# SBUF places of a hybrid attention kernel: small tiles collected in pools of their own, tables padded, 280-column weights spread

## The chip, the core and the metric

The kernel runs on one core of a Trainium2 chip. The core has a matrix engine (TensorE, called PE in the profile; the loading of its stationary operand is shown apart as PEld), three elementwise engines (VectorE = DVE, ScalarE = ACT, GpSimd = POOL) and DMA queues, most of which are issued here from SyncE (SP). All work on SBUF, a memory of 128 partitions; a tile takes the same byte range in every partition, and "place" below means the first byte of a tile, or of a slice of it, within its partition. Matmul results go to PSUM. The metric is device time in microseconds (us) from launch to end, the median of several executions.

## What is computed

One layer of a decoder trunk in float32, 1024 tokens of width 1024. Cut to its steps:

```python
h = rmsnorm(x, norm_mix)
q, kc, vc, ks, vs, kw, vw, nsa_g, rq, rk, rv, rg, gate_a, gate_b = split(h @ w_in)
A = nsa(...)        # compressed + selected + sliding-window attention, gated per head
B = retention(...)  # chunkwise recurrent, per-head norm, swish gate
x = x + (sigmoid(gate_a) * (A @ w_proj_a) + sigmoid(gate_b) * (B @ w_proj_b)) @ w_out
x = x + relu(rmsnorm(x, norm_mlp) @ w_up) ** 2 @ w_down
y = rmsnorm(x, norm_final)
```

## The kernel before

**Matmuls.** Every float32 matrix is split into a high and a low part of type fp32r (`wh`, `wl` for weights; `bh`, `bl` for the transposed activations), and a product is three matmuls: high·high, high·low, low·high. All go through the helper `mm` (L156, its instruction is L157), whose second argument is the stationary operand (loaded into the array) and whose third is the moving one (streamed, up to 512 columns). Before each matmul PE loads the stationary 128x128 block. While one matmul streams, the next one's load runs.

**Stages, in the order of time.** The names in brackets are the PSUM tiles by which the profile's rows tell the stages apart.

- Normalization, retention projections and retention, twice four column groups (`mm`, and small ones `pS`, `pO`, `pD`, `pZ`): `dense_tok` (L218) holds `bh`/`bl` stationary and streams weights of 512 columns. Then the keys and values of attention (w_kva, 512 columns; w_kvb, 280 columns) and the queries (w_q, 512), also `mm`, with the compression matmuls `pc` between them.
- Attention (`S` scores, `pt` transposes of the probabilities, `O` the value products of 256 columns), interleaved with the merge gates (`gps`, weights stationary, `bh`/`bl` moving). The order here is a list of pieces with due times (L934 to L953).
- Projections of A and B (`mm` of L1010; moving tiles `Ah`, `Al`, `Bh`, `Bl`, weights stationary).
- Output product (`mmu` with `bh`/`bl` stationary and w_out moving), with the transposes that form the input of the MLP.
- MLP up (`mmu`, seven products for a pair of blocks in `up_rest`; weights stationary; moving `bh`, `bl` and the sums `t2h`..`t4l`).
- MLP down (`mmd`, `three`, L1294; both operands are `wh`/`wl` tiles of the weight ring).

PE takes its instructions in the order in which they are written. The other engines' lists are ordered by the tile framework. Weights come by DMA into `raw` (3 buffers, L160), are copied to `wh` on ACT and the rest subtracted into `wl` on DVE (`split_w` L181, `split_t1024` L1027).

**Places.** Pools are stacked from the low end of SBUF, some (`side="right"`) from the high end. A tile's size is rounded up to 32 bytes, so a small tile shifts all that is stacked above it. In the build of the kernel before, the 128-column identity `ident` starts at byte 16512, and behind it stand the small tiles `small`, `nhalf`, `gcol`, `ssx` and `rr` (224 bytes with rounding); `raw` therefore starts at 17248. `cret` (2848 bytes), `cmp_m` (480 bytes) and the score scratch tiles `sums`, `mx`, `cf` shift what stands above them again. `chunk_weights` (L228) packs two weight blocks of n columns next to each other; for n = 280 the second block starts 1120 bytes behind the first.

Byte address of the matmul operands modulo 256, from the allocations of the two builds (slices step by multiples of 256 bytes except the packed 280-column blocks):

| operand | before | after |
|---|---|---|
| `bh`, `bl`, `t2h`..`t4l`, `KKs`, `KKw`, `KKc`, `Vs`, `Vw`, `Vc`, `qkT` (right side) | 224 | 224 |
| weights `wh`, `wl` in the ring of the whole kernel, and in the rings of the later stages | 96 | 224 |
| weights `wh`, `wl` in the retention ring (`wrx`) and the compression ring | 128 | 224 |
| second 280-column block in a 96 ring, in a 128 ring | 192, 224 | 224 |
| `Ah`, `Al`, `Bh`, `Bl` | 96 | 224 |
| `QQ`, `ql`, `pS`, `pW` | 64 | 224 |
| `ph`, `pl` | 192 | 224 |
| `ident`, retention tiles (`qk`, `s`, `v`, `sd`, `n`, `z`), compression tiles (`xh`, `xl`, `w2d`, `hh`) | 128 | 224 |
| x rows that are transposed for the MLP (`x1t`), `AT` | 96 | 224 |

Of the 5552 fp32r matmuls with 512 columns, the two operands of 1728 agree modulo 256 before (384 of the projections and 1344 of MLP down, all at 96), and those of 3824 don't: 1152 `mm` of `dense_tok`, 768 `gps`, 176 `S`, 384 `mmu` of the output product, 1344 `mmu` of MLP up. After, the operands of all 7879 PE instructions agree, at 224.

Of the kernel before, what the change touches and what calls it, by code (L numbers as in the profile page):

```python
# [9 lines left out]
F32 = mybir.dt.float32  # L10
F32R = mybir.dt.float32r
I32 = mybir.dt.int32
AF = mybir.ActivationFunctionType
OP = mybir.AluOpType
# [3 lines left out]
P = 128  # L18
S = 1024
D = 1024  # L20
NT = S // P
KD = D // P
# [90 lines left out]
def hybrid_block(ctx: ExitStack, tc: tile.TileContext, a: dict, out: bass.AP):  # L113
    nc = tc.nc
    V, A, G, T = nc.vector, nc.scalar, nc.gpsimd, nc.tensor
    ctx.enter_context(tc.manual_schedule(engines={mybir.EngineType.PE}))

    cst = ctx.enter_context(tc.tile_pool(name="cst", bufs=1, reuse_waits="tile"))
    dram = ctx.enter_context(tc.tile_pool(name="scr", bufs=1, space=DRAM))
    bigs = ctx.enter_context(ExitStack())  # L120
    big = bigs.enter_context(tc.tile_pool(name="big", bufs=1, side="right", reuse_waits="tile"))
    wraw = ctx.enter_context(tc.tile_pool(name="wraw", bufs=3, reuse_waits="tile"))
# [8 lines left out]

    bh = big.tile([P, KD, S], F32R, name="bh")
    bl = big.tile([P, KD, S], F32R, name="bl")
    ident = cst.tile([P, P], F32, name="ident")
    small = cst.tile([P, 16], F32, name="small")
    nhalf = cst.tile([P, 4], F32, name="nhalf")
    gcol = cst.tile([P, KD], F32, name="gcol")
    ssx = cst.tile([P, 2, NT], F32, name="ssx")
    rr = cst.tile([P, NT], F32, name="rr")
    V.memset(nhalf, -0.5)  # L140
    clock = {"t": 0, "n": 0}
    due = []
# [13 lines left out]
    def mm(o, w, m, start, stop):  # L156
        T.matmul(o, w, m, start=start, stop=stop)  # L157

    def load_raw(src, shape):
        r = wraw.tile([P, 1024], F32, name="raw", tag="raw")  # L160
        n = int(np.prod(shape))
        v = r[:, :n]
        if len(shape) == 2:
            v = v.rearrange("p (a b) -> p a b", a=shape[0])
        nc.sync.dma_start(v, src)
        return r[:, :n], n
# [6 lines left out]
    def new_slot(pool=None):  # L173
        if pool is None:
            pool = ring["pools"][ring["i"] % len(ring["pools"])]
            ring["i"] += 1
        h = pool.tile([P, 1024], F32R, name="wh", tag="wh")
        l = pool.tile([P, 1024], F32R, name="wl", tag="wl")
        return h, l

    def split_w(src, shape, eng=None, pool=None):  # L181
        r, n = load_raw(src, shape)
        h, l = new_slot(pool)
        A.activation(h[:, :n], r, AF.Copy)
        (eng or V).tensor_tensor(l[:, :n], r, h[:, :n], op=OP.subtract)  # L185
        return h, l
# [41 lines left out]
    def chunk_weights(name, n, s0=0, s1=4):  # L228
        per = 2
        W = []  # L230
        for s in range(s0, s1):
            h, l = split_w(a[name][:, s * per:(s + 1) * per, :], (per, n))
            for e in range(per):
                W.append((h[:, e * n:(e + 1) * n], l[:, e * n:(e + 1) * n]))
        return W

    with ExitStack() as es:
        psA = es.enter_context(tc.tile_pool(name="psA", bufs=2, space=PSUM, reuse_waits="tile"))
        tabs = es.enter_context(tc.tile_pool(name="tabs", bufs=1, reuse_waits="tile"))
        cret = tabs.tile([P, P + 512 + 72], F32, name="cret")  # L240
        cosr = tabs.tile([P, NT, 64], F32, name="cosr")
        sinr = tabs.tile([P, NT, 64], F32, name="sinr")
        cosn = tabs.tile([P, NT, 8], F32, name="cosn")
# [5 lines left out]
        with ExitStack() as e1:  # L249
# [150 lines left out]
            with tc.manual_schedule(engines={mybir.EngineType.PE, mybir.EngineType.Pool}):  # L400
# [9 lines left out]
                W = chunk_weights("w_r0a", 512, 0, 1)  # L410
# [24 lines left out]
            for c in range(2):  # L435
                rt = {}
                for j in range(NT):
# [21 lines left out]
                    if j == NT - 1:  # L459
                        W = chunk_weights(f"w_r{c}b", 512)  # L460
# [4 lines left out]
                for j in range(NT):  # L465
                    ps = psA.tile([P, 512], F32, name="mm", tag="mm")
                    dense_tok(ps, j, W, 0, 4)
                    if j == 0:
                        s = ret_s(0, qkT)
# [8 lines left out]
                    if j == NT - 1:  # L478
                        W = chunk_weights("w_kva" if c else "w_r1a", 512)
                    v, y = ret_v(j, ps)  # L480
                    cur = (j, c, qkT, s, v, y)
                    if j + 1 < NT:
                        qkT = qkTn
                        s = ret_s(j + 1, qkT)
# [32 lines left out]
        with ExitStack() as e2:  # L517
# [157 lines left out]
            for j in range(2, NT):  # L675
                ps = psA.tile([P, 512], F32, name="mm", tag="mm")
                dense_tok(ps, j, W)
                if j == NT - 1:
                    W = chunk_weights("w_kvb", 280)
                kva_post(j, ps)  # L680
            for j in range(NT):
# [5 lines left out]
                if j == NT - 1:  # L687
                    W = chunk_weights("w_q", 512)
                n = tmp.tile([P, 512], F32, name="n")[:, :256]
# [13 lines left out]
            for i, j in enumerate(reversed(range(NT))):  # L703
# [6 lines left out]
                n = tmp.tile([P, 512], F32, name="n")  # L710
# [56 lines left out]
    with ExitStack() as e3:  # L767
        msk = e3.enter_context(tc.tile_pool(name="msk", bufs=1, reuse_waits="tile"))
# [2 lines left out]
        psO = e3.enter_context(tc.tile_pool(name="psO", bufs=1, space=PSUM, reuse_waits="tile"))  # L771
        at = e3.enter_context(tc.tile_pool(name="at", bufs=2, reuse_waits="tile"))
        edge_m = msk.tile([P, 640], F32, name="edge_m")
        cmp_m = msk.tile([P, 120], F32, name="cmp_m")
        nc.sync.dma_start(edge_m, a["c_edge"])
        nc.sync.dma_start(cmp_m, a["c_cmp"])
        nc.sync.dma_start(gcol, a["norm_mlp"].rearrange("o (k p) -> p (o k)", p=P))
# [17 lines left out]
        def scores(qb, g, hp, u):  # L795
            QQ, ql = qs[qb, g]
            nk, nw = qb + 1, min(qb + 1, 5)
            cS, cW = nk * P, nw * P
            w0 = (nk - nw) * P
            u.update(nk=nk, nw=nw, P=[])  # L800

            def mask(c0, n, width, edge):
                if c0 + n == width:
                    return edge_m[:, 640 - n:]
                return edge_m[:, :n] if edge else edge_m[:, P:P + 1].to_broadcast([P, n])

            for i in range(2):
                h = hp * 2 + i
                sums = at.tile([P, 5], F32, name="sums", bufs=4)
                mx = at.tile([P, 5], F32, name="mx", bufs=4)  # L810
                pS = at.tile([P, 1024], F32, name="pS", bufs=PS_S)
                pW = at.tile([P, 768], F32, name="pW", bufs=PS_S)
                G.memset(pW[:, 704:], 0.0)
                for base, KK, start, width, p in ((1, KKs, 0, cS, pS), (2, KKw, w0, cW, pW)):
                    groups = []
                    for c0 in range(0, width, 512):
                        n = min(512, width - c0)
                        groups.append([(base if c0 == 0 else base + 2, KK, start + c0, n,
                                        mask(c0, n, width, base == 2), p[:, c0:c0 + n])])
                    split = len(groups) > 1  # L820
                    if base == 2:
                        tail = (0, KKc, 0, 64, cmp_m[:, 56 - 8 * qb:120 - 8 * qb], pW[:, 640:704])
                        if groups[-1][0][3] <= 448:
                            groups[-1].append(tail)
                        else:
                            groups.append([tail])
                    exps = []
                    for gi, grp in enumerate(groups):
                        ps = psS.tile([P, 512], F32, name="S")
                        off = 0  # L830
                        done = []
                        for b, K, c0, n, mk, o in grp:
                            done.append((b, ps[:, off:off + n], mk, o))
                            off += n
                        _, K, c0 = grp[0][:3]
                        mm(ps[:, :off], QQ[:, h], K[:, g, c0:c0 + off], True, False)
                        mm(ps[:, :off], ql[:, h], K[:, g, c0:c0 + off], False, True)
                        for b, sc, mk, o in done:
                            V.tensor_tensor_reduce(sc, sc, mk, -0.125, BIGPOS, OP.add, OP.min, mx[:, b:b + 1])  # L839
                            exps.append((b, sc, o))  # L840
                        if gi < len(groups) - 1:
                            yield
                    if split:
                        V.tensor_tensor(mx[:, base:base + 1], mx[:, base:base + 1], mx[:, base + 2:base + 3],
                                        op=OP.min)
                    for b, sc, o in exps:
                        m = b - 2 if b > 2 else b
                        A.activation(o, sc, AF.Exp, bias=mx[:, m:m + 1], scale=-1.0, accum_out=sums[:, b:b + 1])  # L848
                    if base == 1:
                        yield  # L850
                if cS > 512:
                    V.tensor_add(sums[:, 1:3], sums[:, 1:3], sums[:, 3:5])
                cf = at.tile([P, 3], F32, name="cf", bufs=4)
                V.reciprocal(cf, sums[:, :3])
                hd = g * 4 + hp * 2 + i
                V.tensor_mul(cf, cf, gts[:, qb, hd * 3:hd * 3 + 3])  # L856
                for b, v in ((1, pS[:, :cS]), (2, pW[:, :cW]), (0, pW[:, 640:704])):
                    G.tensor_scalar(v, v, cf[:, b:b + 1], 1.0, op0=OP.mult, op1=OP.mult)  # L858
                u["P"].append((pS, pW))
                yield  # L860
# [95 lines left out]
    with ExitStack() as e4:  # L956
# [40 lines left out]
        for i in range(8):  # L997
            h, l = pw[i]
# [56 lines left out]
    with ExitStack() as e5:  # L1055
# [40 lines left out]
        def up_first(X, ticks=False):  # L1096
            p1 = headp.tile([P, 512], F32, name="p1")
            A.activation(p1, prod(X[11], 11, ticks), AF.Copy)
            return {"p1": p1}
# [7 lines left out]
        with ExitStack() as e6:  # L1107
# [44 lines left out]
            W = out_w(0)  # L1152
            for c in range(2):
                cs = slice(c * 512, (c + 1) * 512)
                order = (0, 1, 4, 2, 5, 3, 6, 7) if c else range(NT)
                for n, j in enumerate(order):
# [4 lines left out]
                    if c == 0 and n == NT - 1:  # L1161
                        W = out_w(1)
# [71 lines left out]
        s = heads[0]  # L1234
        for p in range(16):
# [8 lines left out]
            if p < 15:  # L1244
                up_weights(p + 1, nra, nX)
                X = nX
                s = heads[1] if p == 0 else up_first(X)
# [90 lines left out]
    for step, n in enumerate((1, 2, 7, 6, 5, 4, 3)):  # L1338
# [12 lines left out]
        for i in range(4):  # L1351
            b = bank[i]
# [83 lines left out]
```

## Time and profile before

| | us |
|---|---|
| median of 3 runs (1617.21 to 1617.77) | 1617.59 |
| the profiled execution | 1619.48 |
| its span, first to last instruction | 1617.7 |

| engine | busy us | share of the span |
|---|---|---|
| PE | 1576.0 | 97% |
| PEld | 1307.3 | 81% |
| DVE | 1070.7 | 66% |
| ACT | 731.8 | 45% |
| POOL | 436.5 | 27% |

A row of a group reads: line, engine, operation, what it writes `<-` what it reads, shapes, `xcount | busy us, mean ns of one | idle time of the engine before them`. Matmuls are pipelined: each lasts longer than the distance to the next, so the busy time of PE overlaps itself, and the pace is read from how many start in a stretch. The view of stretches gives, for each engine, busy us and in brackets the number of its instructions. `PEclk` is the granted share of PE's full clock.

### The profile page before, as it was taken

The numbers are of one execution on the slowest core, as the hardware profiler recorded it, in microseconds if no ns is written. First come the engines' busy times: TensorE is split into PE (matmuls) and PEld (weight loads), VectorE is DVE, ScalarE is ACT, GpSimd is POOL, SyncE is SP. The second block draws the span as 40 slices with busy tenths as digits, with TensorE's granted clock in tenths as the row PEclk, the third lists the DMA queues.
The fourth block names the chain that finished last, engine by engine and source line by source line (L and its number), as shares of the span: only waits on it lengthen the run. The fifth ranks groups of instructions, "written<-read, shape, count | busy, mean of one in ns | idle before, by whom it ended". The sixth has DMA issues, their size and how long they took to land.

```text
span 1617.7 us, 22741 instructions
## 1 busy us (share of the span) xinstructions
PE 1576.0 (97%) x7879; PEld 1307.3 (81%) x7879; DVE 1070.7 (66%) x2170; ACT 731.8 (45%) x1627; POOL 436.5 (27%) x516
## 2 busy tenths in 40 slices
PE   7999999999999999999999998999999999999997
PEld 5888888887888888888788876888888878888886
DVE  4765564573777777776655367777667657885683
ACT  5454454573677766676522233222222234443442
POOL 4211010001232323333000013644555426621320
PEclk7999999999999999999999999999999999999999
DMA  6112101252111111121544322444444498674472
GB/s 213 50 36 66 52 18 43 66 182 67 49 47 34 53 46 53 47 60 60 182 144 156 109 94 74 160 144 145 152 153 150 160 332 286 207 230 126 132 269 101
DMA packets 98915, 191.83 MB, mean 119 GB/s; under 512 B 26928, under 2 KB 29360, under 8 KB 98800
## 3 DMA queue, kind: packets, MB, share of 16 engines
q1 hardware_dynamic: 98240, 188.55, 35.8%
q0 software_dynamic: 560, 1.84, 0.3%
q8 instruction: 62, 1.02, 0.3%
q14 instruction: 53, 0.43, 0.1%
HBM read 140.02 MB, written 50.33 MB: 118 GB/s over the span
## 4 chain that ended last, share of the span: by engine, by line
PE 83%; DVE 5%; ACT 4%; issue 3%; POOL 2%; DMA 2%; SPq 0%; POOLq 0%; ACTq 0%; DVEq 0%
PE mmu L157 23%; PE mm L157 20%; PE mmd L157 18%; PE gps L157 8%; PE S L157 4%; PE O L157 3%; PE pt L894 2%; PE pt L893 2%; ACT pW L848 1%; DVE S L839 1%; DVE pl L896 1%; PE pO L157 1%; PE pc L157 1%; ACT pS L848 1%; DVE wl L185 0%
## 5 line engine op out<-in xcount | busy, mean ns | idle before, releaser
L1030 DVE TENSOR_TENSOR wl<-raw,wh 128x1024 fp32r<-128x1024 f32 x121 | 182.8, 1535 | 68.5 <-ACT wh L1029 68.3
L1029 ACT ACTIVATE wh<-raw 128x1024 fp32r<-128x1024 f32 x121 | 125.2, 1056 | 217.8 <-PE mmd L157 131.3
L157 PE MATMUL mm<-wh,bh 128*128 128x512 f32 (+1 forms) x448 | 177.1, 395 | 1.0 <-ACT n L581 1.0
L157 PE MATMUL mm<-wh,bl 128*128 128x512 f32 (+1 forms) x448 | 172.7, 385 | 4.7 <-DVE bl L211 4.7
L157 PE MATMUL mmd<-wl,wh 128*128 128x512 f32 x448 | 174.6, 390 | 1.6 <-DVE wl L1030 1.6
L157 PE MATMUL mmd<-wh 128*128 128x512 f32 x448 | 174.5, 390 | 0.9 <-DVE u L1216 0.9
L157 PE MATMUL mmd<-wh,wl 128*128 128x512 f32 x448 | 174.5, 389 | 0.0
L157 PE MATMUL mm<-wl,bh 128*128 128x512 f32 (+1 forms) x448 | 172.1, 384 | 0.1
L896 DVE TENSOR_TENSOR pl<-pt,ph 128x512 fp32r<-128x512 f32 (+1 forms) x160 | 103.8, 649 | 30.2 <-ACT ph L895 27.8
L895 ACT ACTIVATE ph<-pt 128x512 fp32r<-128x512 f32 (+1 forms) x160 | 90.3, 567 | 55.0 <-PE pt L894 51.0
L839 DVE CUSTOM_DVE_ANT_0 S<-S,edge_m 128x512 f32<-128x512 f32 (+3 forms) x192 | 100.7, 530 | 14.7 <-PE S L157 12.7
L157 PE MATMUL gps<-bh,wh 128*128 128x512 f32 x256 | 108.5, 424 | 0.3 <-ACT gst L751 0.2
L858 POOL TENSOR_SCALAR pS<-pS,cf 128x1024 f32<-128x1024 f32 (+7 forms) x64 | 47.8, 748 | 220.2 <-DVE cf L856 71.4
L157 PEld LDWEIGHTS mm<-wh,bl 128*128 128x128 f32 x448 | 85.2, 190 | 22.9 <-DVE bl L211 5.7
L157 PE MATMUL mmu<-bh,wh 128*128 128x512 f32 x256 | 101.3, 396 | 0.0
L157 PE MATMUL mmu<-bl,wh 128*128 128x512 f32 x256 | 101.1, 395 | 0.0
L157 PE MATMUL mmu<-bh,wl 128*128 128x512 f32 x256 | 100.9, 394 | 0.0
L157 PE MATMUL gps<-bh,wl 128*128 128x512 f32 x256 | 100.9, 394 | 0.0
L157 PE MATMUL gps<-bl,wh 128*128 128x512 f32 x256 | 100.7, 393 | 0.0
L157 PEld LDWEIGHTS mmd<-wl,wh 128*128 128x128 f32 x448 | 84.1, 188 | 19.4 <-DVE wl L1030 2.0
L157 PEld LDWEIGHTS mmd<-wh 128*128 128x128 f32 x448 | 84.1, 188 | 18.5 <-issue 1.3
L157 PEld LDWEIGHTS mmd<-wh,wl 128*128 128x128 f32 x448 | 84.1, 188 | 17.5
(312 smaller groups left out, 3975.3 us busy)
## 6 DMA issues: line engine op xcount, KB each, us to landing
raw<-u_scr SPq DMA_DIRECT2D x56, 512.0 KB, 3.9
raw<-w_down SPq DMA_DIRECT2D x41, 512.0 KB, 4.7
raw<-w_up SPq DMA_DIRECT2D x32, 512.0 KB, 3.6
u_scr<-u SPq DMA_DIRECT2D x60, 256.0 KB, 2.3
u_scr<-s SPq DMA_DIRECT2D x45, 256.0 KB, 2.1
y<-w_down SPq DMA_DIRECT2D x16, 512.0 KB, 6.7
x<-x SPq DMA_DIRECT2D x8, 512.0 KB, 3.9
qt<-q_scr SPq DMA_DIRECT2D x32, 128.0 KB, 2.5
```

What stands on the lines that cost most here:

```text
L157: T.matmul(o, w, m, start=start, stop=stop)
L839: V.tensor_tensor_reduce(sc, sc, mk, -0.125, BIGPOS, OP.add, OP.min, mx[:, b:b + 1])
L848: A.activation(o, sc, AF.Exp, bias=mx[:, m:m + 1], scale=-1.0, accum_out=sums[:, b:b + 1])
L858: G.tensor_scalar(v, v, cf[:, b:b + 1], 1.0, op0=OP.mult, op1=OP.mult)
L893: T.transpose(tp[:, bi * 2], p0, ident)
L894: T.transpose(tp[:, bi * 2 + 1], p1, ident)
L895: A.activation(ph[:, :n], tp[:, :n], AF.Copy)
L896: V.tensor_sub(pl[:, :n], tp[:, :n], ph[:, :n])
L1029: A.activation(h[:, :n], r, AF.Copy)
L1030: V.tensor_sub(l[:, :n], r, h[:, :n])
```

## The change

It adds two pools ahead of all others: `few` for `small`, `nhalf`, `gcol`, `ssx`, `rr`, and `smp` for the four buffers of `sums`, so that these stand ahead of `ident`. `cret` is padded from 712 to 768 columns and `cmp_m` from 120 to 128, and only their old columns are used. `cf` is allocated next to `mx`. `chunk_weights` loads the two blocks of 280 columns into the two halves of its tile (2048 bytes apart) instead of next to each other; for 512 columns it gives the same slices as before.

```diff
+    few = ctx.enter_context(tc.tile_pool(name="few", bufs=1, reuse_waits="tile"))
+    smp = ctx.enter_context(tc.tile_pool(name="smp", bufs=4, reuse_waits="tile"))
     cst = ctx.enter_context(tc.tile_pool(name="cst", bufs=1, reuse_waits="tile"))
...
+    small = few.tile([P, 16], F32, name="small")
+    nhalf = few.tile([P, 4], F32, name="nhalf")
+    gcol = few.tile([P, KD], F32, name="gcol")
+    ssx = few.tile([P, 2, NT], F32, name="ssx")
+    rr = few.tile([P, NT], F32, name="rr")
     ident = cst.tile([P, P], F32, name="ident")
-    small = cst.tile([P, 16], F32, name="small")
-    nhalf = cst.tile([P, 4], F32, name="nhalf")
-    gcol = cst.tile([P, KD], F32, name="gcol")
-    ssx = cst.tile([P, 2, NT], F32, name="ssx")
-    rr = cst.tile([P, NT], F32, name="rr")
...
         for s in range(s0, s1):
-            h, l = split_w(a[name][:, s * per:(s + 1) * per, :], (per, n))
+            r = wraw.tile([P, 1024], F32, name="raw", tag="raw")
+            r, h, l = (t.rearrange("p (a b) -> p a b", a=per)[:, :, :n] for t in (r, *new_slot()))
+            nc.sync.dma_start(r, a[name][:, s * per:(s + 1) * per, :])
+            A.activation(h, r, AF.Copy)
+            V.tensor_tensor(l, r, h, op=OP.subtract)
             for e in range(per):
-                W.append((h[:, e * n:(e + 1) * n], l[:, e * n:(e + 1) * n]))
+                W.append((h[:, e], l[:, e]))
...
-        cret = tabs.tile([P, P + 512 + 72], F32, name="cret")
+        cret = tabs.tile([P, 6 * P], F32, name="cret")[:, :P + 512 + 72]
...
-        cmp_m = msk.tile([P, 120], F32, name="cmp_m")
+        cmp_m = msk.tile([P, P], F32, name="cmp_m")[:, :120]
...
-                sums = at.tile([P, 5], F32, name="sums", bufs=4)
+                sums = smp.tile([P, 5], F32, name="sums")
                 mx = at.tile([P, 5], F32, name="mx", bufs=4)
+                cf = at.tile([P, 3], F32, name="cf", bufs=4)
...
-                cf = at.tile([P, 3], F32, name="cf", bufs=4)
                 V.reciprocal(cf, sums[:, :3])
```

The change moves no instruction: on every engine the built lists of the two kernels have the same instructions in the same order. In them, the four loads of w_kvb, their four copies on ACT and their four subtractions on DVE have the form 128x2x280 in place of 128x560, and one RECIPROCAL on DVE waits for one semaphore fewer while one subtraction of L976 waits for one more, on DVE itself.

## The prediction

> **What bounds the kernel now.** I read the page from the top: the shares of the engines, the chain that ended last, then the groups and the stretches of each stage.
>
> ```profile
> span 1617.7 us, 22741 instructions
> PE 1576.0 (97%) x7879; PEld 1307.3 (81%) x7879; DVE 1070.7 (66%) x2170; ACT 731.8 (45%) x1627; POOL 436.5 (27%) x516
> PEclk7999999999999999999999999999999999999999
> PE 83%; DVE 5%; ACT 4%; issue 3%; POOL 2%; DMA 2%; SPq 0%; POOLq 0%; ACTq 0%; DVEq 0%
> ```
>
> PE is busy for 97% of the span, 83% of the chain that ended last is PE, and its clock is full in every slice but the first. So the pace at which matmuls follow each other sets the time, in most stages directly. The next question is whether that pace is the same in all stages. Three stretches hold nothing on PE but 512-column matmuls of one kind: the first is MLP up, the second MLP down, the third the projections. The number behind PE's busy time counts what ran in them.
>
> ```profile
> 1010.00:1300.00 290.00, 290.00 (x1249) 235.37 (x1249) 205.85 (x241) 65.01 (x73) 145.35 (x104) 1.00 0.46 154
> 1310.00:1600.00 290.00, 289.74 (x1278) 240.05 (x1279) 205.71 (x169) 119.82 (x142) 95.30 (x42) 1.00 0.64 209
> 795.00:878.00 83.00, 83.00 (x367) 68.50 (x366) 50.33 (x71) 19.79 (x26) 0.00 (x0) 1.00 0.48 151
> ```
>
> The clock is 1.00 in all three. MLP up starts one matmul every 290/1249 = 232.2 ns, MLP down one every 290/1278 = 226.9, the projections one every 83/367 = 226.2. DVE and DMA are at least as busy in MLP down as in MLP up (205.71 against 205.85 us, DMA 0.64 against 0.46), so load on the other engines doesn't explain why the slower stage is slower. The table of places does: MLP down and the projections are the two stages whose operands agree modulo 256, at 96; in MLP up the weights stand at 96 and the moving operand at 224. The single matmuls show it too (least, median and longest duration in ns, at PSUM tiles `mm` of the projections, `mmd` and `mmu`):
>
> ```profile
> L157 PE MATMUL mm<-Al,wh x64: 388/389/390, 795.2 to 879.1; 128*128 128x512 f32 x64
> L157 PE MATMUL mmd<-wh,wl x448: 388/389/396, 1303.3 to 1609.1; 128*128 128x512 f32 x150
> L157 PE MATMUL mmu<-t3l,wh x64: 392/393/397, 1003.5 to 1292.9; 128*128 128x512 f32 x64
> ```
>
> Every matmul on `t3l` lasted longer (392 at least) than every one on `Al` (390 at most). In both the weights are stationary in the ring at 96 and a tile of the same shape streams. I take it that the loading of a stationary block and the streaming matmul beside it disturb each other when their places differ modulo 256, and cost each other about 5 ns per matmul.
>
> [...] That it is the place remains an inference; the rival below gets its chance for it.
>
> **The sum, stage by stage.** The saving of one matmul is its distance now less 226.9 ns. For the other stages the chain that ended last gives unbroken runs (start, duration, line and number of matmuls), from the retention projections, the keys and values, the first gate and the output product:
>
> ```profile
> 51.39 5.58 PE mm L157 x24
> 57.84 5.57 PE mm L157 x24
> 143.50 5.64 PE mm L157 x24
> 244.34 5.66 PE mm L157 x24
> 267.87 4.19 PE mm L157 x18
> 286.58 4.20 PE mm L157 x18
> 385.56 5.59 PE gps L157 x24
> ...
> 889.93 5.57 PE mmu L157 x24
> 895.94 5.58 PE mmu L157 x24
> 901.96 5.60 PE mmu L157 x24
> 907.99 5.59 PE mmu L157 x24
> ```
>
> - `dense_tok` with 512 columns, 1152 matmuls: the six `mm` runs are 30.84 us for 132, 233.6 ns each, so 6.7 ns saved, 1152 x 6.7 = 7.7 us. In these stages little but PE stands on the chain, so I count all of it.
> - Gates and 512-column scores, 768 + 176 matmuls: 5.59/24 = 232.9 ns, 6.0 ns saved, 5.7 us. Attention isn't PE alone. Its chain (shares of the stretch from 390 to 782 us) and its waits:
>
> ```profile
> by line: PE gps L157 32.1%; PE S L157 14.7%; PE O L157 12.9%; PE pt L894 7.4%; PE pt L893 6.7%; ACT pW L848 4.5%; DVE S L839 4.0%; DVE pl L896 3.4%; issue 2.9%; ACT pS L848 2.4%; ACT ph L895 1.8%; POOL pS L858 1.6%; PE pt L784 1.5%; DVE mx
> L894 PE MATMUL pt<-ident,pS 128*128 128x128 f32 x144 | 36.3, 276 | 4.3 <-POOL pS L858 4.3
> ```
>
>   The five large PE terms and the transposes of L784 make 75%; in the rest PE waits for the softmax on ACT, DVE and POOL (the 4.3 us are one such wait), and a faster PE waits longer there. I count 75% of 5.7 us, 4.3 us.
> - Output product, 384 matmuls: the four `mmu` runs are 22.34 us for 96, 232.7 ns, 5.8 saved, 2.2 us. Towards its end the chain passes through the elementwise work that forms the MLP's input, where matmuls run beside it:
>
> ```profile
> by line: PE mmu L157 42.3%; POOL y L1140 7.1%; DVE t4l L1114 6.9%; DVE bl L1114 4.5%; issue 4.3%; DVE f L1138 3.9%; DVE y L1123 3.8%; PE tp L1119 3.1%; ACT t4h L1113 2.7%; DVE t3l L1114 2.7%; DVE x1t L1163 2.6%; DVE t2l L1114 2.4%; ACT t3h
> ```
>
>   That is the stretch from 940 to 1010 us; with under half of it on `mmu`, some 40 us of the stage, about 170 matmuls, keep half of their 1.0 us. I count 1.7 us.
> - MLP up, 1344 matmuls: 232.2 less 226.9 is 5.3 ns, 7.1 us. It passes on in full: DVE works 205.85 of 290 us in that stage, and stays below PE when the stage is 2% shorter.
> - Projections and MLP down, 1728 matmuls, agree already: 0.
>
> Together 7.7 + 4.3 + 1.7 + 7.1 = **20.8 us**.
>
> **Edits and operations that I count at nothing.** The value products have 256 columns, with `ph`/`pl` at 192 and the values at 224 now; nothing in the trace shows them in agreement. The compression products, in agreement at 128, and two kinds of fp32 transposes (128 against 64, and 128 against 128) are the nearest rows:
>
> ```profile
> L157 PE MATMUL O<-ph,Vs 128*128 128x256 f32 x144 | 38.8, 281 | 0.0
> L157 PE MATMUL pc<-wl,xh 128*128 128x256 f32 x32 | 9.0, 283 | 0.0
> L893 PE MATMUL pt<-ident,pS 128*128 128x128 f32 x144 | 36.2, 272 | 0.0
> L390 PE MATMUL pZ<-ident,z 128*128 128x128 f32 x32 | 6.1, 271 | 0.0
> 305.41 0.29 PE L157 MATMUL mm<-wh,bh 128*128 128x280 f32 x1
> 305.81 0.29 PE L157 MATMUL mm<-wh,bh 128*128 128x280 f32 x1
> 306.20 0.29 PE L157 MATMUL mm<-wh,bh 128*128 128x280 f32 x1
> 306.58 0.29 PE L157 MATMUL mm<-wh,bh 128*128 128x280 f32 x1
> ```
>
> `O` may lose the 2 ns by which `pc` lasts longer (592 x 2 = 1.2 us more) or gain as much as a 512-column gate (592 x 6.0 = 3.6 us less). I take 0, since the 280-column matmuls, in threes of four different places and in agreement in some of them, all run at 0.38 to 0.40 us for three. For the same reason those 192 count as 0 (192 x 6 = 1.2 us at most), and the transposes, 272 and 271 ns, too.
>
> The split load of w_kvb keeps its bytes and has pieces half as long. It stands well ahead of its use: its last three issues are at 245 to 252 us, its subtractions at 296 to 298.5 us, and the first 280-column matmul starts behind them.
>
> ```profile
> 245.52 6.21 SPq L165 DMA_DIRECT2D raw<-w_kvb  x3
> 295.96 1.39 DVE L185 TENSOR_TENSOR wl<-raw,wh 128x560 fp32r<-128x560 f32 x2 [1.09 <-ACT wh L184]
> 298.82 0.38 PE L157 MATMUL mm<-wh,bh 128*128 128x280 f32 x1
> raw<-w_kvb SPq DMA_DIRECT2D x4, 280.0 KB, 3.1
> ```
>
> Its landing of 3.1 us is hidden by 44 us. The subtraction in two pieces of 280 would be felt only if the three ended over 0.3 us later; the number of elements stays, and at worst it costs a few tenths of a us. The pools, the padding and the earlier `cf` issue nothing and move no instruction; the one wait added (DVE for DVE, in the projections' weights) is for work ahead of it on its own engine.
>
> **The forecast.** The profiled execution took 1619.48 us, its span is 1617.7, and the median of the runs shown is 1617.59, 0.1% below the profiled one. The saving is a matter of counts, so I take it off the median: 1617.6 - 20.8 = 1596.8, rounded to **1597 us**.
>
> **Rivals.**
> - *Only long unbroken runs gain.* In attention three gate matmuls alternate with scores and transposes, and the chain row above shows ACT and DVE steps between them; then its 4.3 us and the 1.7 of the output product are given back as waits on `pS` and `x1t`: 1617.6 - 14.8 = 1602.8. Chance 0.15.
> - *More than forecast.* Attention and output product pass on all (1.4 + 0.5 us more) and `O` gains its 3.6: 1597 - 5.5 = 1591.5. Chance 0.10.
> - *The places don't matter.* The 5 ns belong to the stages in some other way, and the change does nothing: 1617.6. [...] Against it stand the `t3l` and `Al` rows. Chance 0.06.
> - *Slower: 224 is the slow place, and agreement has nothing to do with it.* Every slow row above has one operand at 224 and no fast row has any; the trace has no long run of 512 columns with both there. Then the slow stages stay as they are, and MLP down and the projections, 1728 matmuls that now have none at 224, pay the 5.3 ns: 1617.6 + 9.2 = 1626.8. It decides as soon as the distance in MLP down is over 227.5 ns or so. Against it: `mm` rows have the moving operand at 96 or 128 and `mmu` the stationary one, with the same 233 ns, which a bad place of one operand would have to give for either side alike. Chance 0.05.
>
> The forecast keeps 0.64. The granted clock is below full in one late stretch, beside the pauses at the end of the output product:
>
> ```profile
> 950.00:1010.00 60.00, 50.79 (x213) 39.83 (x212) 46.56 (x59) 23.73 (x41) 19.18 (x13) 0.94 0.21 71
> ```
>
> That is 0.06 x 60 = 3.6 us of lost clock, and since the pauses move, I put 2 us either way for it. With that, the range from 1591 to 1606 holds the first three cases but for their edges. Faster by over 0.2%, which is about what a measurement of this kernel can tell from no change, has 0.89, within 0.2% 0.06, slower 0.05.
>
> **What would show it.** Right: 227 to 227.5 ns per matmul in the MLP up stretch as well, runs of 24 `mm` and `gps` in 5.45 us, `t3l` rows with a median of 389 or 390, MLP down unchanged. In attention, more idle PE time ahead of `pt<-ident,pS` shows the part given back. Wrong: MLP up still at 232 ns (the places don't matter), or MLP down above 227.5 ns (224 is slow).

## The result: 0.75% faster, a little more than half of what was forecast

| | runs | median us | lowest to highest |
|---|---|---|---|
| before | 4 | 1617.4 | 1615.42 to 1617.77 |
| after | 4 | 1605.2 | 1603.16 to 1606.18 |

The ratio is 0.9925 (95% interval 0.9908 to 0.9943), so the change saves 12.2 us where 20.8 were forecast. The 1605.2 us lie inside the stated range of 1591 to 1606, but only by 0.8 us. The profiled execution of after took 1606.18 us. Its page first: span, shares of the engines, the clock in 40 slices, the chain that ended last.

```profile
span 1604.4 us, 22741 instructions
PE 1560.5 (97%) x7879; PEld 1302.9 (81%) x7879; DVE 1070.4 (67%) x2170; ACT 731.7 (46%) x1627; POOL 435.5 (27%) x516
PEclk8999999999999999999999999999999999999999
PE 83%; DVE 5%; ACT 4%; issue 3%; POOL 2%; DMA 2%; SPq 0%; POOLq 0%; ACTq 0%; DVEq 0%
```

The shares are those of before, to a per cent; PE's busy time fell by 15.5 us and that of its weight loads by 4.4, the others by 1.0 at most. So nothing new bounds the kernel. Nor did the clock change: 0.991 of full is granted over the whole span in both profiles. The two long stretches, MLP up and MLP down (busy us and in brackets how many started), and the single matmuls (least, median, longest in ns):

```profile
1010.00:1280.00 270.00, 270.00 (x1193) 223.56 (x1192) 198.00 (x228) 62.92 (x71) 141.75 (x101) 1.00 0.44 154
1310.00:1580.00 270.00, 270.00 (x1193) 223.57 (x1192) 192.29 (x160) 112.76 (x134) 93.90 (x40) 1.00 0.63 207
```

```profile
L159 PE MATMUL mmu<-t3l,wh x64: 387/389/389, 997.5 to 1279.7; 128*128 128x512 f32 x64
```

270/1193 is 226.3 ns in both: MLP up now runs at the pace of MLP down, and the `t3l` matmuls, 392 ns at least before, last 389 at most.

The two built programs hold the same instructions in the same order, so the profiled executions can be laid side by side. For each stage, the table takes the start of its first matmul, after less before, and gives how much of that difference arose in the stage. The first row ends at the first run of 24 dense matmuls, at 51.1 us in before. The last column repeats it for `e7_packed` below, which is the changed kernel but for one stage.

| stage | forecast us | after | e7_packed |
|---|---|---|---|
| start, up to the first run of 24 | 0 | -1.9 | -2.4 |
| retention, keys and values with 512 columns | -7.7 with the queries | -2.4 | -2.2 |
| keys and values with 280 columns | 0 | 0.0 | +0.2 |
| queries | (above) | -0.7 | -0.7 |
| attention with gates | -4.3 | -0.6 | -0.7 |
| projections | 0 | +0.8 | +0.5 |
| output product | -1.7 | -1.4 | -1.4 |
| MLP up | -7.1 | -7.2 | -6.8 |
| MLP down to the end | 0 | 0.0 | 0.0 |

MLP up came out as forecast, and the output product nearly so. What is missing is in the retention projections (4.7 us short, with the queries) and in attention (3.7 us short). The first row is not put down to the change: the first transposes wait for `h`, for which DVE stands idle until the first transfers land (6.97 us for `pos_i` in before, 5.68 in after), and they started at 9.65 us in before, 8.36 in after, 9.65 in `e2_left96`, 8.94 in `e6_ret_runs_before`, 7.63 in `e3_gate_runs` and 7.70 in `e4_gate_runs_before`, early and late with either kind of places.

Where PE waits was not the answer. In attention, the projections and the output product its longest waits (us in all, times, longest) are those of before to a few tenths. Two of before, then four of after:

```profile
PE tp L1119 <- DVE x1t L1163: 4.6, 3, 1.9
PE pt L894 <- POOL pS L858: 4.3, 7, 1.8
```

```profile
PE tp L1125 <- DVE x1t L1169: 4.8, 3, 2.0
...
PE pt L900 <- POOL pS L864: 4.5, 7, 1.8
...
PE S L159 <- ACT pS L855: 2.1, 4, 0.9
PE mm L159 <- ACT Bh L986: 1.8, 2, 1.7
```

The wait for `pS` grew by 0.2 us. Take as a delay every distance in attention that is over 100 ns above the median of its kind (the same tiles, operands and widths, worked out from the trace): what these lie above it comes to 12.5 us before and 12.8 after. If the gates had become 6 ns faster and the gain had been given back in waits, this would have grown by several us. (Most of the projections' 0.8 us is such a wait, though: PE comes earlier to `Bh` and `Bl`, and waits 1.8 + 0.4 us there instead of 1.4 + 0.2.) The distances themselves show the cause. PE's timeline of after in the retention stage (start us, duration, what):

```profile
118.60 0.39 PE L159 MATMUL mm<-wh,bh 128*128 128x512 f32 x1
118.83 0.39 PE L159 MATMUL mm<-wl,bh 128*128 128x512 f32 x1
119.05 0.39 PE L159 MATMUL mm<-wh,bl 128*128 128x512 f32 x1
...
119.73 0.39 PE L159 MATMUL mm<-wh,bl 128*128 128x512 f32 x1
119.96 0.57 PE L159 MATMUL pS<-qkT 128*128 128x256 f32 x4
120.37 0.45 PE L159 MATMUL mm<-wh,bh 128*128 128x512 f32 x1
120.66 0.40 PE L159 MATMUL mm<-wl,bh 128*128 128x512 f32 x1
120.89 0.40 PE L159 MATMUL mm<-wh,bl 128*128 128x512 f32 x1
...
121.59 0.39 PE L159 MATMUL mm<-wh,bl 128*128 128x512 f32 x1
```

The matmuls of 119.28 and 119.51, and of 121.13 and 121.36, are left out here. From 118.60 to 119.73 five matmuls take 1.13 us, 226 ns each. Then four short products `pS` come between, and from 120.66 to 121.59 four matmuls of the same stage, kind and places take 0.93 us, 232.5 each. Grouped over all 512-column matmuls from 45 to 380 us by their position in a run that nothing else interrupts (mean ns to the next start, worked out from the trace; distances over 260 ns, which hold a wait or the step from another kind of product, are left out):

| position | 2 | 3 | 4 | 5 | 6 | 7 | 8 | 9 | 10 | 11 and later |
|---|---|---|---|---|---|---|---|---|---|---|
| before | 232.8 | 233.1 | 232.4 | 231.9 | 234.7 | 233.5 | 232.6 | 233.1 | 233.4 | 232.9 |
| after | 233.5 | 232.1 | 233.4 | 227.0 | 230.4 | 232.7 | 228.1 | 230.2 | 229.3 | 226.7 |

Before, the distance doesn't depend on the position. After, it is back and forth between 227 and 234 ns for some ten matmuls, and then stays at 226.7. In this stretch only 394 of 937 distances counted are at position 11 or later, and the mean went from 232.9 to 229.2 ns. The chain that ended last shows the same (start, duration, line, number):

```profile
49.52 5.49 PE mm L159 x24
55.88 5.46 PE mm L159 x24
...
133.00 5.54 PE mm L159 x24
141.03 5.51 PE mm L159 x24
...
240.81 5.55 PE mm L159 x24
...
380.66 5.46 PE gps L159 x24
...
884.91 5.47 PE mmu L159 x24
```

The first gates, which follow 54 matmuls of the queries without a break, come to 5.46 us for 24, 227.5 ns; the runs of the output product come to 5.47 to 5.50. The `mm` runs stand between there and the 5.58 to 5.66 us of before, since each has to settle anew. In attention 218 of the 228 runs of gates are threes between other matmuls (the chain from 400 to 440 us, two rows of before and three of after: start, duration, line, number):

```profile
404.01 0.70 PE gps L157 x3
...
436.16 0.69 PE gps L157 x3
```

```profile
401.05 0.69 PE gps L159 x3
...
413.42 0.69 PE gps L159 x3
...
415.49 0.69 PE gps L159 x3
```

These rows read 0.69 to 0.72 us in both kernels, and the mean over the 512-column matmuls from 400 to 780 us went from 233.0 to 232.3 ns only.

### The profile page after: what moved, and what is told of

The parts are those of the page before. It is cut to its first block, busy times and chain, and to the rows that moved or that the text cites. A ratio compares the mean times of both kernels' runs of the same rounds, so it can differ in the third digit from the quotient of the medians.

```text
span 1604.4 us, 22741 instructions
## 1 busy us (share of the span) xinstructions
PE 1560.5 (97%) x7879; PEld 1302.9 (81%) x7879; DVE 1070.4 (67%) x2170; ACT 731.7 (46%) x1627; POOL 435.5 (27%) x516
## 4 chain that ended last, share of the span: by engine, by line
PE 83%; DVE 5%; ACT 4%; issue 3%; POOL 2%; DMA 2%; SPq 0%; POOLq 0%; ACTq 0%; DVEq 0%
PE mmu L159 23%; PE mm L159 19%; PE mmd L159 18%; PE gps L159 8%; PE S L159 4%; PE O L159 3%; PE pt L900 2%; PE pt L899 2%; ACT pW L855 1%; DVE S L846 1%; PE pO L159 1%; DVE pl L902 1%; PE pc L159 1%; ACT pS L855 1%; DMA y<-w_down 0%
## 5 line engine op out<-in xcount | busy, mean ns | idle before, releaser
L1036 DVE TENSOR_TENSOR wl<-raw,wh 128x1024 fp32r<-128x1024 f32 x121 | 178.4, 1499 | 69.2 <-ACT wh L1035 69.2
L846 DVE CUSTOM_DVE_ANT_0 S<-S,edge_m 128x512 f32<-128x512 f32 (+3 forms) x192 | 100.7, 530 | 14.3 <-PE S L159 12.5
```

What stands on the lines that cost most here:

```text
L1036: V.tensor_sub(l[:, :n], r, h[:, :n])
```

## The experiments

The theory that these distances suggest, theory A: the place modulo 256 does set the pace, but the stream of matmuls has to settle, over some ten 512-column matmuls without interruption, and it settles only where the operands agree. Where runs are shorter, the change brings little. The rivals stand in the expectations.

### The pace by itself: `e1_places`

A kernel of matmuls alone: the layer is left out, `x` is copied to the output. Runs of 48 matmuls with chosen places of the two operands follow four transposes each; then come runs of 24 with one kind of interruption between them, and short runs. It was executed once, and all figures are of that execution.

```python
# name, place of the stationary operand, place of the moving one (bytes modulo 512), columns
("eqz", 0, 0, 512), ("eqn", 96, 96, 512), ("eqo", 128, 128, 512), ("eqt", 224, 224, 512),
("da", 0, 16, 512), ("db", 0, 32, 512), ("dc", 0, 64, 512), ("dd", 0, 96, 512), ("de", 0, 128, 512),
("df", 0, 160, 512), ("dg", 0, 192, 512), ("dh", 0, 224, 512), ("di", 0, 256, 512),
("dj", 128, 0, 512), ("dk", 96, 224, 512), ("dl", 224, 96, 512),
...
for name, brk in (("none", None), ("fla", lambda: flips(1)), ...,
                  ("shc", lambda: shorts(1, 256)), ..., ("shf", lambda: shorts(1, 512, False)), ...):
    for _ in range(2):
        run("pre", 0, 0, 512, 24)
        if brk:
            brk()
        run(name, 0, 0, 512, 24)
```

> It leaves the whole layer out: x is copied to the output, and PE alone runs rows of 48 fp32r matmuls of 512 columns with the two operands at chosen places (eq..: the same modulo 256, at 0, 96, 128 and 224; d..: 16 to 256 bytes apart), then runs of 24 with something short between them. Theory A (the places must agree modulo 256, and a run needs about ten matmuls after an interruption until it settles): all four eq rows settle at 226 to 227 ns per matmul from about the 11th on, 256 apart as well, all the other distances stay at 231 to 234 throughout; after each kind of interruption the first ten take about 231 on average; rows of three and of six never settle, rows of twelve only at their end. Rival B (the place 224, or a coarser agreement such as modulo 128 or 64, matters): eq rows differ among themselves, or 128 or 64 apart settle too. Rival C (other engines' work disturbs the matmuls in attention and retention, not the interruptions): with PE alone, rows of three run at 227 as well.

Two stretches of it, one with places that agree at 0, one with places 128 apart: PE works alone, at full clock.

```profile
56.00:66.00 10.00, 10.00 (x46) 8.24 (x45) 0.00 (x0) 0.00 (x0) 0.00 (x0) 1.00 0.00 0
148.00:158.00 10.00, 10.00 (x44) 8.11 (x44) 0.00 (x0) 0.00 (x0) 0.00 (x0) 1.00 0.01 2
```

The single matmuls by places (ns, least, median, longest): agreeing at 0, 96 and 224, 256 apart, 64 apart, 128 apart, 32 apart.

```profile
L54 PE MATMUL eqz<-mv,st x48: 387/389/477, 55.5 to 66.3; 128*128 128x512 f32 x48
L54 PE MATMUL eqn<-mv,st x48: 387/389/482, 66.9 to 77.7; 128*128 128x512 f32 x48
L54 PE MATMUL eqt<-mv,st x48: 389/389/482, 89.6 to 100.4; 128*128 128x512 f32 x48
L54 PE MATMUL di<-mv,st x48: 387/389/473, 193.8 to 204.6; 128*128 128x512 f32 x48
L54 PE MATMUL dc<-mv,st x48: 388/392/482, 124.2 to 135.0; 128*128 128x512 f32 x48
L54 PE MATMUL de<-mv,st x48: 390/393/476, 147.3 to 158.3; 128*128 128x512 f32 x48
L54 PE MATMUL db<-mv,st x48: 392/395/477, 112.5 to 123.6; 128*128 128x512 f32 x48
```

The median is the settled duration; it is 389 in each of the rows whose places agree modulo 256 (at 0, 96 and 224, and 256 apart), and 392 to 395 in the other three. The distances from start to start, from the trace (first twelve of a run, then the mean of the later ones):

```
eqt 224/224          319 231 236 228 233 230 227 226 227 227 227 226 | 226.7
di  256 apart        313 229 233 236 224 231 236 228 232 231 227 226 | 226.7
dc   64 apart        321 235 232 231 226 229 232 225 230 232 226 228 | 228.9
da   16 apart        310 234 235 230 228 234 235 230 227 235 235 230 | 231.7
dk  128 apart        315 232 228 230 233 241 232 230 233 228 230 233 | 232.3
dl  128 apart        322 229 238 228 238 229 238 228 239 229 237 229 | 233.5
db, dd, df, dg, dh: 32, 96, 160, 192, 224 apart                      | 233.2 to 234.3
none (no interruption)          227 227 227 226 227 227 226 226 228 226 227 226
fla (one transpose)             314 229 233 237 224 231 235 229 232 231 227 226
shc (one of 256 columns)        232 236 228 233 231 226 226 228 226 227 227 226
shf (one of 512, not agreeing)  225 228 226 227 226 227 227 227 226 227 227 226
```

The agreeing runs settle at 226.7 within eleven matmuls, the others don't within their 48, with no other engine at work. So rival B has it wrong: neither the place 224 (389 ns, as at 0 and 96) nor agreement modulo 64 or 128 (228.9 ns at 64 apart, 232.3 at 128) is what counts. After one product of 256 columns, five matmuls take 232 ns in the mean before the stream is settled again: a gate of three, in attention between such products and transposes, ends before that. Runs of twelve and of three between four transposes, 128 apart (`d`) and agreeing (busy us, mean ns of one):

```profile
L54 PE MATMUL twelved<-mv,st 128*128 128x512 f32 x144 | 36.5, 402 | 0.0
L54 PE MATMUL twelve<-mv,st 128*128 128x512 f32 x144 | 36.1, 400 | 0.0
...
L54 PE MATMUL threed<-mv,st 128*128 128x512 f32 x36 | 11.4, 425 | 0.0
L54 PE MATMUL three<-mv,st 128*128 128x512 f32 x36 | 11.1, 417 | 0.0
```

From the start of one row of twelve to that of the next, transposes included, it is 3203 ns agreeing and 3233 ns 128 apart (mean, the first row left out). That is 2.5 ns for each matmul, about half of the settled 5.7 ns (232.4 less 226.7); the runs of 12 and 24 in the retention stage gained 3.7.

The rows of three go less well with theory A. They don't settle: the last distance of a row is 231 to 235 ns. Yet they gain, from 1140 to 1128 ns for a row, 4 ns for each matmul, where the threes of attention gained 0.7. So the length of the run alone doesn't say what a short run gains. Here the transposes between the rows are the same for both kinds of row and PE works alone; in the kernel the products between the threes moved as well, and three other engines work. Which of these makes the difference, no run separates, and rival C isn't put aside for the threes. For long runs it is: MLP up settles while DVE is busy for 198 of 270 us.

### The low side of SBUF back at 96: `e2_left96`

The only edit undoes the collecting of `sums`. By the allocations of its build, the low side moves back from 224 to 96, all 512-column operands among it, so that the same 3824 fp32r matmuls disagree as before. The expectation below has everything on the low side at 96; the tiles above `sums` in its old pool (`pS`, `pW`, `ph`, `pl`) in fact stay at 224, so the value products `O` agree as in the changed kernel. The padding, the other pool and the spread columns stay.

```diff
-    smp = ctx.enter_context(tc.tile_pool(name="smp", bufs=4, reuse_waits="tile"))
...
-                sums = smp.tile([P, 5], F32, name="sums")
+                sums = at.tile([P, 5], F32, name="sums", bufs=4)
```

> The changed kernel with the score scratch tile sums back in its old pool: everything on the low side of SBUF moves back by 128 bytes, to 96 modulo 256, the high side stays at 224; the padding and the spread columns stay. Theory A: MLP up goes back to 232 ns per matmul (7 us), the output product gives 1.4 and the projections for retention 2 to 3 us back: 1615 to 1617 us. Rival B (224 as such is what was gained, or padding): no more than half of it comes back, under 1610.

1617.38 us (1615.44 to 1619.37), 0.9992 of before (0.9982 to 1.0002): the whole gain is gone with 128 bytes. The MLP up stretch and its `t3l` matmuls:

```profile
1010.00:1280.00 270.00, 270.00 (x1164) 218.99 (x1163) 194.79 (x226) 60.61 (x68) 137.97 (x98) 1.00 0.43 150
```

```profile
L158 PE MATMUL mmu<-t3l,wh x64: 392/393/397, 1005.3 to 1294.6; 128*128 128x512 f32 x64
```

1164 in place of 1193 matmuls in 270 us, 232.0 ns each, and the rows are those of before. Weights at 96 and a moving operand at 224 do this; the other edits carry nothing by themselves, nor does the agreement of `O`.

### Gates in long runs: `e3_gate_runs` and `e4_gate_runs_before`

If the length of the runs is what keeps attention from gaining, gates in runs of 24 must gain in full. The same edit is made to the changed kernel and to the kernel before: a gate piece no longer gives way after three matmuls, and the list of how many pieces stand ahead of each step is cut accordingly.

```diff
-GATES = [8] + [8] * 16 + [6] * 12 + [7, 7, 7, 7]
+GATES = [1] * 17 + [1, 1, 1, 0] * 4
...
-GATE0 = 8
+GATE0 = 1
...
-            if k < KD - 1:
-                yield
```

> The changed kernel with the gates of attention given out in whole runs of 24 matmuls in place of threes. Theory A: the gate matmuls settle after ten, their mean goes from 230.5 to about 228.6 ns, 1.5 us less in 768 of them, and what softmax then waits behind a run of 5.5 us comes on top: between 3 us less and some us more in all. Rival C: the mean stays at 230 to 231 ns within the runs too, from first to last.

> The kernel before with the same runs of 24 gate matmuls. Theory A: with the operands at 96 and 224 they never settle, 232 to 233 ns from first to last, whatever the length of the run; the time differs from e3 by more than before and changed kernel differ now (12 us), by 13 to 15 us. Rival C: the same distance in both kernels.

The two took 1727.24 us (1725.35 to 1729.09) and 1740.34 us (1737.78 to 1744.03). Both are far slower than the kernels they come from, 1.067 and 1.0758 of before, far beyond what was expected of the softmax. PE's waits in the first say why (us, times, longest): with the gates gone from between the steps of a softmax, nothing is left to run while it works.

```profile
PE pt L898 <- POOL pS L862: 40.5, 24, 5.4
PE S L159 <- ACT pS L853: 23.9, 16, 1.9
PE O L159 <- DVE pl L900: 11.8, 16, 1.6
```

With the pauses the granted clock fell too, to 0.977 and 0.982 of full over the spans of the two profiles, against 0.991; by estimate from that, 0.014 of 1724.8 us, it cost the first some 24 us.

The waits are the same with either set of places (40.2, 23.5 and 11.2 us in the other), so the difference of the pair, 13.1 us, is still that of the places. Gates in the chain that ended last, of `e3_gate_runs`, then of `e4_gate_runs_before` (start, duration, number):

```profile
413.68 5.45 PE gps L159 x24
433.08 5.47 PE gps L159 x24
455.21 5.45 PE gps L159 x24
```

```profile
416.73 5.58 PE gps L157 x24
...
458.69 5.58 PE gps L157 x24
478.00 5.59 PE gps L157 x24
```

5.45/24 is 227.1 ns, 5.58/24 is 232.5. The 5.45 us is what was forecast for the gates of the changed kernel, and a gate reaches it when it isn't cut into threes. By position the 512-column distances from 400 to 880 us are 229 to 234 in `e3_gate_runs` up to the fifth and 227 to 228 from the sixth on; in `e4_gate_runs_before` they are 231 to 235 at every position. Other engines were at work during these runs of gates; the first run of `e3_gate_runs` (us busy of 5.40: PE, PEld, DVE, ACT, POOL):

```profile
413.70:419.10 5.40, 5.40 (x25) 4.46 (x25) 1.47 (x7) 1.98 (x6) 2.19 (x3) 1.00 0.00 0
```

### Retention projections in whole runs: `e5_ret_runs` and `e6_ret_runs_before`

The same for the retention stage: in the second half of each column group the 24 matmuls of a token tile stay together, and the small products come behind them.

```diff
-                    dense_tok(ps, j, W, 0, 4)
+                    if j + 1 < NT:
+                        qkTn = ret_t(j + 1)
+                    dense_tok(ps, j, W)
...
-                    if j + 1 < NT:
-                        qkTn = ret_t(j + 1)
...
-                    dense_tok(ps, j, W, 4, 8)
```

> The changed kernel with the second half of each retention group in whole runs: the 24 matmuls of a token tile stand together, with the transposes for the next tile ahead of them and the small retention matmuls behind, in place of 12 + 12 with the small ones between. Theory A: one start from scratch less in each of 16 tiles; over its first ten such a start costs 30 to 40 ns, so 0.5 to 0.6 us less in all, and matmuls 11 to 24 of these runs at 226.7 ns. As small a gain can be eaten by a wait for the small matmuls' operands, so the time itself stays within 3 us of the changed kernel. Rival C (the neighbours on other engines disturb): no settling in the second half of the longer runs, 229 ns throughout.

> The kernel before with the same order of retention as e5. Theory A: 232 to 234 ns from the first to the last matmul of the runs of 24, since the operands stand 128 and 96 bytes apart; the time differs from the kernel before only by what the order itself does, and from e5 by 12 to 14 us.

1617.93 us (1614.49 to 1620.22) and 1633.42 us (1631.07 to 1634.09). The expectation of the first was missed: it is 13 us slower than the changed kernel, since PE now reaches the transposes of `z` before `z` is there. Counted as above, the delays from 45 to 380 us come to 16.7 us, against 3.0 in the changed kernel; the granted clock there, 0.98 of full against 1.00, is part of them. The largest wait of the stretch:

```profile
PE pZ L396 <- DVE z L389: 8.6, 3, 5.1
```

The places gain 15.5 us between the two, against 12.2 between the kernels in their own order. That is more than the 12 to 14 us expected, and more than the 0.5 to 0.6 us extra of theory A; the spreads (1614.49 to 1620.22 and 1631.07 to 1634.09) are too wide to tell 15.5 from 13. The distances say it more closely. The mean distance from 45 to 380 us is 228.6 ns in the first (226.7 from position 11 on, which 478 of 896 reach, against 394 of 937 in the changed kernel) and 232.9 in the second: 4.3 ns gained in place of 3.7, which over these 900 distances is 0.5 us, as theory A has it. Only the order costs more than longer runs bring.

### The 280-column blocks packed again: `e7_packed`

The changed kernel with w_kvb loaded and split as before, its second block 1120 bytes behind the first.

```diff
-            r = wraw.tile([P, 1024], F32, name="raw", tag="raw")
-            r, h, l = (t.rearrange("p (a b) -> p a b", a=per)[:, :, :n] for t in (r, *new_slot()))
-            nc.sync.dma_start(r, a[name][:, s * per:(s + 1) * per, :])
-            A.activation(h, r, AF.Copy)
-            V.tensor_tensor(l, r, h, op=OP.subtract)
+            h, l = split_w(a[name][:, s * per:(s + 1) * per, :], (per, n))
             for e in range(per):
-                W.append((h[:, e], l[:, e]))
+                W.append((h[:, e * n:(e + 1) * n], l[:, e * n:(e + 1) * n]))
```

> The changed kernel with the two 280-column blocks of w_kvb packed next to each other again, so that the second one stands at 64 in place of 224 modulo 256. Theory A: e1 ran 280 columns at 127.8 ns in agreement and at 128.9 ns 128 bytes apart, so half of 192 matmuls lose 1.1 ns, 0.1 us: the same time as the changed kernel. Rival: the spread columns carry a part of the gain, over 1 us slower than the changed kernel in the stage of w_kvb (27.9 us from its first to its last matmul in both kernels now).

1605.11 us (1603.83 to 1605.94), 0.993 of before (0.9914 to 0.9947): the time of the changed kernel. In its profile the 280-column stage differs from before by +0.2 us, in the changed kernel's by 0.0. The spread columns are worth nothing that can be seen here.

No version that was run is faster than the changed kernel by more than the spread of its runs.

## Why the prediction was right in sign and short in size

That the measured time fell into the stated range is in part luck: the range reached up to 1606 for the clock beside the pauses and for the rival of 1602.8 us, and neither the clock nor that rival's waits are what kept the time up. The account, term by term:

- **What bounds the kernel.** Right. PE's pace sets the time; the time fell by what the pace gained, the shares of the engines stayed, and no other engine became the bound.
- **The place is the cause.** Right, and shown twice: by `e2_left96`, where 128 bytes take the whole gain away, and by `e1_places`, where PE works alone and the place alone makes 226.7 or 231.7 to 234.3 ns (228.9 at 64 apart). The forecast's picture of it, that the load of a stationary block and the stream beside it disturb each other, was not tested; the runs show the places and the pace, not the way from one to the other.
- **MLP up, 7.1 us.** Right: 7.2 in the profiled execution, and the distance is that of MLP down, 226.3 ns in both stretches. Its runs are long.
- **Output product, 1.7 us.** Near in size: 1.4. Laid side by side, its matmuls gained 4.1 ns and not 5.8, since each run of 24 has to settle anew: 384 x 4.1 = 1.6 us. Of the half microsecond that the end of the stage was to give back, 0.2 went to the wait for `x1t` (4.8 us, 4.6 before).
- **Retention, keys and values, queries, 7.7 us.** The step that failed: 6.7 ns saved by each of 1152 matmuls. The settled distance was carried from MLP down, one long unbroken run, to runs of 12 and 24 between short products. Part of the 6.7 was not there before either: 233.6 ns was read from six runs of the chain, and the mean over all distances counted is 232.9. The matmuls gained 3.7 ns in the mean, 1152 x 3.7 = 4.3 us at most; 3.0 us came out in the profiled execution. The trace of before already held a sign of it, in a stage whose operands agree: in the projections, after a short hold-up at 797.7 us, the distances are 329, 337, 236, 228, 233 and 231 ns before they come to 227 and 226. The mean of 226.2 ns that the prediction took from that stage hides this, since such starts are rare in it.
- **Attention, 4.3 us.** The same step failed harder: 6.0 ns for each of 944 matmuls. They gained 0.7 ns in the mean, 944 x 0.7 = 0.7 us, and 0.6 came out. The 75% that were to pass on were not the error: the delays grew by 0.3 us in all, so there was nothing to give back. That the gates can have the full gain in longer runs is shown by the pair of gate kernels (227.1 against 232.5 ns). Why threes gain even less here than the 4 ns of the rows of three in `e1_places` stays open.
- **What was counted at nothing.** `O`, the transposes and the 280-column matmuls: right (`O<-ph,Vs` 281 ns in the mean before and 280 after, `pt<-ident,pS` 272 and 276 in both, the 280-column stage 0.0 us); the spread of the columns is shown to carry nothing. The projections lost 0.8 us, most of it to the waits for `Bh` and `Bl`, which the forecast left out.
- **The rivals.** "Only long unbroken runs gain" named part of the cause, but expected the loss as waits in attention and the output product, and the full 7.7 us in retention; both are refuted. That 224 is the slow place is refuted by `e1_places` (`eqt` 389, as at 0 and 96) and by MLP down, unchanged at 224. That the places don't matter is refuted by the time itself.
- **What would show it.** MLP up and `t3l` showed it right, MLP down too. The `mm` runs came to 5.46 to 5.55 us, not to 5.45. Runs of 24 `gps` in 5.45 us came in the experiment; in the changed kernel the first run has 5.46, and the others are cut into threes. The idle time ahead of `pt<-ident,pS`, which was to show what is given back, grew by 0.2 us only.

Some of the size stays open. The sum of the stages without the start is 11.5 us in after's profile and 11.2 in that of `e7_packed`, the medians are 12.2 us apart (some 9 to 15 by the interval), and the profiled executions can't tell these apart. Why the stream takes some ten matmuls to settle, and why 256 bytes apart is as good as the same place (226.7 ns both), no run here shows.

## What to carry to other kernels

A pace that was measured in one long run of equal matmuls holds for such runs (226.7 ns settled, 229.2 in the mean from 45 to 380 us); before it is carried to a stage that interleaves short products, look in the fast stage at the distances that follow each of its own interruptions, and count how many matmuls the slow stage has in a row. For streams of 512-column fp32r matmuls, operands at the same place modulo 256 bytes were worth about 2.5% here where runs are long (226.3 in place of 232.2 ns in MLP up), and cost nothing but padding. Making runs longer to get it can cost far more than it brings, when the short products were what covered another engine's work (1727.24 us for `e3_gate_runs`, 1605.2 for the changed kernel).

## What the runs showed of the hardware that was not expected

- The settling itself: 4 to 11 matmuls after one to four transposes (a run of 24 then takes 5.46 to 5.49 us, and 5.44 without an interruption), some 6 after one product of 256 columns or twelve of 280 (5.46 to 5.47), none after a single 512-column matmul whose places don't agree (5.44), 3 to 4 after twelve of those (5.45 to 5.46; all in `e1_places`). Rows of three, which don't settle, still gain 4 ns for each matmul between the same transposes (1128 in place of 1140 ns for a row).
- In `e1_places`, 64 bytes apart lies between agreement and the rest (228.9 ns), 256 apart counts as agreement (226.7), 16 apart doesn't (231.7).
- For narrower matmuls the sign isn't the same (`e1_places`): 384 columns 173.3 ns agreeing and 176.0 at 128 apart, 280 columns 127.8 and 128.9, but 256 columns 120.0 agreeing and 118.7 at 128 apart. That fits with value products of 256 columns that gained next to nothing in the kernel (`O<-ph,Vs` 281 ns in the mean before, 280 after).
